# A hybrid encoder trunk: on-chip tiles in a new order, TensorE's operands first and at multiples of 2 KB

## The chip, the cores and the metric

One core of one Trainium2 chip. The metric is device time of one execution in microseconds, as the median of several runs. The kernel and its reference compute in float32; products are made of two float32r parts (a high part and the remainder), which TensorE multiplies.

## The reference

Two layers over 256 tokens of width 1,024. What bears on the time is the chain of matrix products:

```python
def hybrid_layer(x, layer_idx, norm1_g, w_in, ...):
    h = rms_norm(x, norm1_g)
    proj = jnp.einsum('bsd,de->bse', h, w_in)        # 1024 x 10000
    ...
    y_a = mlstm_branch(aq, ak, av, ao, ag, a_conv_w, a_gate_bias, a_norm_g)
    y_b = gqa_branch(bq, bk, bv, b_qnorm_g, b_knorm_g)
    y_c = natten_branch(cq, ck, cv, c_rpb)
    y_d = diff_branch(dq, dk, dv, d_lq1, d_lk1, d_lq2, d_lk2, d_subln_g, lambda_init)
    g = jax.nn.sigmoid(gl.astype(F32)).reshape(bsz, s, N_BRANCH, D_MODEL)
    merged = (g[:, :, 0] * (y_a @ w_up_a) + g[:, :, 1] * (y_b @ w_up_b)
              + g[:, :, 2] * (y_c @ w_up_c) + g[:, :, 3] * (y_d @ w_up_d))
    x = x + merged.astype(dt) @ w_out
    h2 = rms_norm(x, norm2_g)
    ffn = (jax.nn.silu(h2 @ w_ffn_gate) * (h2 @ w_ffn_up)) @ w_ffn_down   # 2816 wide
    return x + ffn
```

After the second layer comes a last RMSNorm.

## The kernel before

All weights come from one array in the order in which they are used (`unit_order`, line 57), in units of 128 x 2,048 float32 that are loaded as halves of 128 x 1,024. A half is loaded by SP's queue into one of four `raw` tiles (`load_next`, line 242), copied by ScalarE with rounding to float32r into one of five `whi` tiles (`emit_hi`, line 258), and VectorE subtracts to leave the remainder in one of five `wlo` tiles (`emit_lo`, line 265). The activations are kept transposed in the same two parts: `xT` (line 208) holds the normalised input as [part, 8 k-slices, 256 tokens], so that its 128 x 128 slices lie 512 bytes apart in a partition; the `yt_` tiles (line 190) do the same for the branches' results and the hidden layer of the feed-forward part.

A product is `mm3` (line 357): high x high, high x low, low x high, three matmuls that add up in one bank. The activation slice is the stationary operand and 512 columns of `whi` or `wlo` are the moving one. `blk512` (line 371) goes over the four k-slices of each unit for both halves of the tokens; `ffn_gu` and `ffn_dn` (lines 1289, 1305) run it over the 11 feed-forward chunks of 256; `bkv_block` (line 1106) multiplies by 272 columns at a time, the first 272 columns of a half and then the next. Between the products small tasks run: transposes on TensorE against `ident`, softmax pieces (`soft_item`, line 739, whose operands are `rq_` and `kb` tiles; `soft_tail`, line 849, with `re_` as moving and `vb` or `vc` as stationary operand), the mLSTM heads (`a_head`, line 604, with `w2_` tiles).

The order of all instructions is written out by the program when it is built. A planner (`Track` and `Meter`, lines 103 to 167) adds up estimated times for each engine, from the shapes of the operands (lines 146 to 156) and from which parts of which tile, by its name and the offset within it, were written or read before (lines 112 to 129). `slot` (line 296) asks it which task may go next. Tiles of the same kind are handed out from lists (`Res`, line 81), oldest free one first. Line 166 is the one place from which `Meter` issues, so nearly every instruction in the profile has that line, and tiles are what tells them apart; the loads have line 240.

All on-chip tiles are declared at the head of `trunk`, lines 186 to 227, and once more at line 447 (`stats`). They take their places in a partition in this order, each beginning at a multiple of 32 bytes:

```python
    W2 = many(8, "w2_", [128, 520])
    K4 = many(4, "k4_", [128, 1024])
    YT = many(3, "yt_", [128, 2, 4, S], F32R)
    ...
    xT = sb("xT", [128, 2, 8, S], F32R)
    ...
    raw = [sb("raw%d" % i, [128, 1024]) for i in range(NRAW)]
    whi = [sb("whi%d" % i, [128, 1024], F32R) for i in range(NH)]
    wlo = [sb("wlo%d" % i, [128, 1024], F32R) for i in range(NH)]
```

Of the kernel before, what the change touches and what calls it, by code (L numbers as in the profile page):

```python
# [12 lines left out]
F32R = mybir.dt.float32r  # L13
BF16 = mybir.dt.bfloat16
# [5 lines left out]
S = 256  # L20
D = 1024
# [149 lines left out]
def trunk(ctx: ExitStack, tc, x_in, wts, par, parc, cst, dist, t2w, fg, out):  # L171
# [8 lines left out]
    def sb(name, shape, dt=F32):  # L180
        return pool.tile(shape, dt, name=name, tag=name)

    def many(n, name, shape, dt=F32):
        return Res([sb("%s%d" % (name, i), shape, dt) for i in range(n)])

    dense = [psp.tile([128, 512], F32, name="pd%d" % i, tag="pd%d" % i) for i in range(3)]
    PS = Res([psp.tile([128, 512], F32, name="pa%d" % i, tag="pa%d" % i) for i in range(5)])
    W2 = many(8, "w2_", [128, 520])
    K4 = many(4, "k4_", [128, 1024])
    YT = many(3, "yt_", [128, 2, 4, S], F32R)  # L190
    RQ = many(2, "rq_", [128, 2, 512], F32R)
    RE = many(3, "re_", [128, 2, 512], F32R)
    T2 = many(2, "t2_", [128, 2, 384])
    SM = many(8, "sm_", [128, 16])
    acc = [sb("acc%d" % i, [128, 2, 512]) for i in (0, 1)]
    EA = Res(acc)
    everyres = [EA, PS, W2, K4, YT, RQ, RE, T2, SM]

    ident = sb("ident", [128, 128])
    make_identity(nc, ident)  # L200
    identr = sb("identr", [128, 36], F32R)
    cs = sb("cs", [128, K_W])
    mA = sb("mA", [128, 384])
    ndist = sb("ndist", [128, 384], BF16)
    mhalf = sb("mhalf", [128, 20])
    lnsc = sb("lnsc", [128, 1])
    x = sb("x", [128, 2, D])
    xT = sb("xT", [128, 2, 8, S], F32R)
    pt = sb("pt", [128, P_W])
    pc2 = [sb("pc%d" % i, [128, C_W]) for i in range(L)]  # L210
    rowz = sb("rowz", [128, 2, 2, 36])
    iz = sb("iz", [128, 2, 36])
    mrow = sb("mrow", [128, 2, S], F32R)
    gcols = sb("gcols", [128, 2, 2, 36])
    gtok = sb("gtok", [128, 32])
    va = sb("va", [128, 2, 4, 129])
    vd = sb("vd", [128, 2, 512])
    vc = sb("vc", [128, 2, 8, 2, 64], F32R)
    vb = sb("vb", [128, 2, 2, 2, 64], F32R)
    ktok = sb("ktok", [128, 2, 128])  # L220
    kb = sb("kb", [128, 2, S], F32R)
    bsm = sb("bsm", [128, 2, 10])
    mvt = sb("mvt", [128, 16])
    NRAW, NH = 4, 5
    raw = [sb("raw%d" % i, [128, 1024]) for i in range(NRAW)]
    whi = [sb("whi%d" % i, [128, 1024], F32R) for i in range(NH)]
    wlo = [sb("wlo%d" % i, [128, 1024], F32R) for i in range(NH)]

    with tc.manual_schedule():

# [6 lines left out]
        def dma(eng, dst, src):  # L237
            state["dma"] = max(state["dma"], track.after(None, [], [dst])) + math.prod(dst.shape) / 94e3
            track.note(None, [], [dst], state["dma"] + 2.3)
            eng.dma_start(dst, src)  # L240

        def load_next():
            h = state["load"]
            if h < nhalf:
                w = width(h)
                dma(nc.sync, raw[h % NRAW][:, :w], wts[h // 2][:, (h % 2) * 1024:(h % 2) * 1024 + w])
                state["load"] += 1
                if h >= NRAW and consts:
                    dma(nc.sync, *consts.pop(0))
# [175 lines left out]
        for _ in range(NRAW - 2):  # L425
            load_next()
        dtile = W2.get()
        consts += [(pt[:, :], par[0]), (cs[:, :], cst), (dtile[:, :384], dist),
# [8 lines left out]
        def tables():  # L437
# [5 lines left out]
            V.tensor_scalar(ndist, dtile[:, :384], -1.0, None, op0=ALU.mult)  # L443
            W2.put(dtile)

# [4 lines left out]
        def boundary_chunk(t, c, gcol, st):  # L450
# [16 lines left out]
            yield  # L467
            while not W2.ok(1):
                yield
            w = W2.get()  # L470
            A.activation(w[:, :512], x[:, t, c * 512:(c + 1) * 512], AF.Square,
                         accum_out=st[:, 2 * c + t:2 * c + t + 1])
            W2.put(w)
            bnd["sq"] += 1
# [24 lines left out]
        def y_up(b, y):  # L499
            while not yt_ok(b):  # L500
                yield
            yt = yt_get(b)
            for t in (0, 1):
                while not PS.ok(1):
                    yield
                p = PS.get()
                for k in range(4):
                    T.transpose(p[:, k * 128:(k + 1) * 128], y[:, t, k * 128:(k + 1) * 128], ident)
                yield
                p4 = p.rearrange("p (k n) -> p k n", k=4)  # L510
                A.activation(yt[:, 0, :, tsl(t)], p4, AF.Copy)
                yield
                sub_lo(yt[:, 1, :, tsl(t)], p4, yt[:, 0, :, tsl(t)])
                PS.put(p)
            yield
            Bs[b]["yt"] = yt
# [87 lines left out]
        def a_head(B, h, pc):  # L604
# [61 lines left out]
            yield  # L666
            while not (PS.ok(2) and ("hb" in B or K4.ok(1))):
                yield
            if "hb" not in B:
                B["hb"] = K4.get()  # L670
            ps = (PS.get(), PS.get())
# [34 lines left out]
        def a_main(B, pc):  # L706
# [28 lines left out]
            yield from y_up("a", hb.rearrange("p (t n) -> p t n", t=2))  # L735
            K4.put(hb)


        def soft_item(B, i, kind):
# [46 lines left out]
            if kind == "c":  # L786
                T2.put(B["t2"].pop(i))
            yield
# [40 lines left out]
            yield  # L829
            while not (PS.ok(1) and "v" in B and ("y" in B or K4.ok(1))):  # L830
                yield
            if "y" not in B:
                B["yraw"] = K4.get()
                B["y"] = B["yraw"].rearrange("p (t n) -> p t n", t=2)
# [14 lines left out]
        def soft_tail(B, i, c, e):  # L849

            while not (PS.ok(1) and RE.ok(1)):
                yield
            p, r = PS.get(), RE.get()
            for kt in (0, 1):
# [16 lines left out]
            for kt, half in ((0, 0), (0, 1), (1, 1), (1, 0)):  # L871
# [3 lines left out]
                else:  # L875
                    T.matmul(p[:, 0:256], v[kt].rearrange("p a n -> p (a n)"), r[:, 0, k2], start=kt == 0, stop=kt == 1)
            RE.put(r)
            yield
# [141 lines left out]
        def c_main(l, B):  # L1020
# [10 lines left out]
            for i in range(4):  # L1031
                while not T2.ok(1):
                    yield
                t2 = T2.get()
                dma(nc.scalar, t2[:, :, :], t2w[l, i])
# [467 lines left out]
```

## Time and profile before

| | |
|---|---|
| median of 3 runs | 1092.74 us (1091.99 to 1093.77) |
| the profiled execution | 1093.29 us |
| its span, first to last instruction | 1091.5 us, 14,727 instructions |
| TensorE, matmuls | busy 1077.9 us (99%), 5,272 instructions |
| TensorE, weight loads | 879.6 us (81%), beside the matmuls |
| VectorE | 765.2 us (70%) |
| ScalarE | 616.8 us (57%) |
| GpSimd | 156.6 us (14%) |
| DMA | 184.8 MB, mean 169 GB/s |

The page gives busy time by engine, the span in 40 slices, the chain of work that ended last and the groups of instructions; the trace answers for a stretch, an engine or a tile. Matmuls overlap in the records: the duration of one runs until its result has left the array, while the next has long begun. How fast they follow one another is seen in the timeline, from one start to a later one with the instructions between them counted.

### The profile page before, as it was taken

The numbers are of one execution on the slowest core, as the hardware profiler recorded it, in microseconds if no ns is written. First come the engines' busy times: TensorE is split into PE (matmuls) and PEld (weight loads), VectorE is DVE, ScalarE is ACT, GpSimd is POOL, SyncE is SP. The second block draws the span as 40 slices with busy tenths as digits, with TensorE's granted clock in tenths as the row PEclk, the third lists the DMA queues.
The fourth block names the chain that finished last, engine by engine and source line by source line (L and its number), as shares of the span: only waits on it lengthen the run. The fifth ranks groups of instructions, "written<-read, shape, count | busy, mean of one in ns | idle before, by whom it ended". The sixth has DMA issues, their size and how long they took to land.

```text
span 1091.5 us, 14727 instructions
## 1 busy us (share of the span) xinstructions
PE 1077.9 (99%) x5272; PEld 879.6 (81%) x5272; DVE 765.2 (70%) x1361; ACT 616.8 (57%) x1095; POOL 156.6 (14%) x130
## 2 busy tenths in 40 slices
PE   9999999999999999999999999999999999999997
PEld 7888887888888888888788888787888888888885
DVE  6689889787556755564576988997965666556555
ACT  7665657775444644444467656686744464444443
POOL 0001345143300000000000006434223000000000
PEclk9999999999999999999999999999999999999999
DMA  8444444545555555545554444345365546564551
GB/s 286 156 163 157 155 135 146 165 135 188 178 175 173 190 192 177 193 171 178 184 166 136 163 166 143 127 165 171 128 200 185 179 169 196 173 206 158 193 182 68
DMA packets 52328, 184.80 MB, mean 169 GB/s; under 512 B 6048, under 2 KB 6432, under 8 KB 52256
## 3 DMA queue, kind: packets, MB, share of 16 engines
q1 hardware_dynamic: 50112, 178.57, 49.1%
q10 hardware_dynamic: 2144, 5.31, 1.6%
q8 instruction: 41, 0.67, 0.2%
q14 instruction: 31, 0.25, 0.1%
HBM read 182.80 MB, written 1.05 MB: 168 GB/s over the span
## 4 chain that ended last, share of the span: by engine, by line
PE 95%; DVE 3%; DMA 1%; issue 0%; ACT 0%; POOLq 0%; POOL 0%; ACTq 0%
PE pd L166 69%; PE pa L166 26%; DVE sm L166 1%; DVE wlo L166 1%; DVE k L166 1%; DMA x<-in_x_dram 1%; DVE rq L166 0%; DVE acc L166 0%; ACT yt L166 0%; DVE mvt L166 0%; ACT pa L166 0%; DVE x L166 0%; ACT k L166 0%; POOLq L1499 0%; POOL st L166 0%
## 5 line engine op out<-in xcount | busy, mean ns | idle before, releaser
L166 PE MATMUL pd<-whi,xT 128*128 128x512 f32 (+1 forms) x1984 | 646.4, 396 | 0.0
L166 DVE TENSOR_TENSOR wlo<-raw,whi 128x1024 fp32r<-128x1024 f32 (+2 forms) x341 | 426.5, 1263 | 113.5 <-ACT whi L166 112.9
L166 PEld LDWEIGHTS pd<-whi,xT 128*128 128x128 f32 x1984 | 372.1, 188 | 85.1
L166 ACT ACTIVATE whi<-raw 128x1024 fp32r<-128x1024 f32 (+2 forms) x341 | 354.1, 1047 | 147.0 <-PE pd L166 95.7
L166 PE MATMUL pd<-wlo,xT 128*128 128x512 f32 (+1 forms) x992 | 389.8, 393 | 0.0
L166 PEld LDWEIGHTS pd<-wlo,xT 128*128 128x128 f32 x992 | 187.0, 188 | 39.4 <-DVE wlo L166 0.3
L166 PE MATMUL pa<-whi,yt 128*128 128x512 f32 x408 | 138.5, 401 | 1.4 <-ACT yt L166 1.4
L166 PEld LDWEIGHTS pa<-whi,yt 128*128 128x128 f32 x408 | 76.6, 188 | 19.6 <-ACT yt L166 1.8
L166 PE MATMUL pd<-whi,yt 128*128 128x512 f32 (+1 forms) x272 | 87.1, 390 | 0.0
L166 PE MATMUL pa<-wlo,yt 128*128 128x512 f32 x204 | 80.5, 394 | 0.0
L166 DVE SCALAR_TENSOR_TENSOR w<-w,pd 128x256 f32<-128x256 f32 x44 | 18.5, 421 | 88.3 <-ACT w L166 88.2
L166 POOL TENSOR_TENSOR st<-st,mhalf 128x2 f32<-128x2 f32 (+1 forms) x6 | 3.9, 654 | 521.2 <-DVE st L166 521.2
L166 ACT ACTIVATE k<-pd,st 128x512 f32<-128x512 f32 (+1 forms) x52 | 31.5, 624 | 58.7 <-PE pd L166 58.7
L166 PEld LDWEIGHTS pd<-whi,yt 128*128 128x128 f32 x272 | 50.7, 188 | 10.9
L166 ACT ACTIVATE w<-pd,st 128x256 f32<-128x256 f32 (+1 forms) x48 | 23.6, 492 | 54.8 <-PE pd L166 52.4
L166 ACT ACTIVATE yt<-pa 128x512 fp32r<-128x512 f32 x34 | 20.3, 597 | 58.6 <-PE pa L166 58.6
L166 PE MATMUL pd<-wlo,yt 128*128 128x512 f32 (+1 forms) x136 | 52.7, 388 | 0.0
L166 PEld LDWEIGHTS pa<-wlo,yt 128*128 128x128 f32 x204 | 38.5, 189 | 7.9
L166 POOL TENSOR_TENSOR w<-w,sm 128x512 f32<-128x512 f32 x32 | 40.5, 1290 | 23.9 <-DVE sm L166 23.9
L166 POOL TENSOR_TENSOR acc<-acc,k 128x512 f32<-128x512 f32 x16 | 30.5, 1907 | 85.0 <-DVE k L166 85.0
L166 DVE TENSOR_TENSOR yt<-pa,yt 128x512 fp32r<-128x512 f32 x30 | 20.6, 688 | 28.9 <-ACT yt L166 28.9
L166 ACT ACTIVATE w<-w,sm 128x256 f32<-128x256 f32 x64 | 31.7, 501 | 11.0 <-DVE sm L166 6.3
(154 smaller groups left out, 1010.8 us busy)
## 6 DMA issues: line engine op xcount, KB each, us to landing
raw<-in_wts_dram SPq DMA_DIRECT2D x332, 512.0 KB, 3.7
t<-in_t2w_dram ACTq DMA_DIRECT2D x8, 384.0 KB, 3.6
raw<-in_wts_dram SPq DMA_DIRECT2D x8, 272.0 KB, 2.9
pt<-in_par_dram SPq DMA_DIRECT2D x1, 584.0 KB, 7.6
pt<-in_par_dram ACTq DMA_DIRECT2D x1, 584.0 KB, 4.6
out_dram<-k SPq DMA_DIRECT2D x2, 288.0 KB, 2.1
x<-in_x_dram ACTq DMA_DIRECT2D x1, 512.0 KB, 9.1
k<-in_fg_dram ACTq DMA_DIRECT2D x1, 512.0 KB, 3.5
```

Source lines behind the costliest of these rows:

```text
L166: return f(out, *a, **k)
```

## The change

The declarations at the head of `trunk` are put in another order. First come three small tiles (`ndist`, `rowz`, `gcols`), then the weights in two parts, `xT`, and the other tiles that TensorE reads, then the larger tiles of the other engines and last the small ones. The `w2_` tiles become 512 columns wide in place of 520. Nothing but declarations is changed.

```diff
     PS = Res([psp.tile([128, 512], F32, name="pa%d" % i, tag="pa%d" % i) for i in range(5)])
-    W2 = many(8, "w2_", [128, 520])
-    K4 = many(4, "k4_", [128, 1024])
+    NRAW, NH = 4, 5
+
+    ndist = sb("ndist", [128, 384], BF16)
+    rowz = sb("rowz", [128, 2, 2, 36])
+    gcols = sb("gcols", [128, 2, 2, 36])
+    whi = [sb("whi%d" % i, [128, 1024], F32R) for i in range(NH)]
+    wlo = [sb("wlo%d" % i, [128, 1024], F32R) for i in range(NH)]
+    xT = sb("xT", [128, 2, 8, S], F32R)
     YT = many(3, "yt_", [128, 2, 4, S], F32R)
     RQ = many(2, "rq_", [128, 2, 512], F32R)
     RE = many(3, "re_", [128, 2, 512], F32R)
+    mrow = sb("mrow", [128, 2, S], F32R)
+    vc = sb("vc", [128, 2, 8, 2, 64], F32R)
+    vb = sb("vb", [128, 2, 2, 2, 64], F32R)
+    kb = sb("kb", [128, 2, S], F32R)
+    vd = sb("vd", [128, 2, 512])
+    acc = [sb("acc%d" % i, [128, 2, 512]) for i in (0, 1)]
+    K4 = many(4, "k4_", [128, 1024])
+    W2 = many(8, "w2_", [128, 512])
+    x = sb("x", [128, 2, D])
+    raw = [sb("raw%d" % i, [128, 1024]) for i in range(NRAW)]
+    ktok = sb("ktok", [128, 2, 128])
+    ident = sb("ident", [128, 128])
     T2 = many(2, "t2_", [128, 2, 384])
     SM = many(8, "sm_", [128, 16])
-    acc = [sb("acc%d" % i, [128, 2, 512]) for i in (0, 1)]
     EA = Res(acc)
     everyres = [EA, PS, W2, K4, YT, RQ, RE, T2, SM]
 
-    ident = sb("ident", [128, 128])
     make_identity(nc, ident)
     identr = sb("identr", [128, 36], F32R)
     cs = sb("cs", [128, K_W])
     mA = sb("mA", [128, 384])
-    ndist = sb("ndist", [128, 384], BF16)
     mhalf = sb("mhalf", [128, 20])
     lnsc = sb("lnsc", [128, 1])
-    x = sb("x", [128, 2, D])
-    xT = sb("xT", [128, 2, 8, S], F32R)
     pt = sb("pt", [128, P_W])
     pc2 = [sb("pc%d" % i, [128, C_W]) for i in range(L)]
-    rowz = sb("rowz", [128, 2, 2, 36])
     iz = sb("iz", [128, 2, 36])
-    mrow = sb("mrow", [128, 2, S], F32R)
-    gcols = sb("gcols", [128, 2, 2, 36])
     gtok = sb("gtok", [128, 32])
     va = sb("va", [128, 2, 4, 129])
-    vd = sb("vd", [128, 2, 512])
-    vc = sb("vc", [128, 2, 8, 2, 64], F32R)
-    vb = sb("vb", [128, 2, 2, 2, 64], F32R)
-    ktok = sb("ktok", [128, 2, 128])
-    kb = sb("kb", [128, 2, S], F32R)
     bsm = sb("bsm", [128, 2, 10])
     mvt = sb("mvt", [128, 16])
-    NRAW, NH = 4, 5
-    raw = [sb("raw%d" % i, [128, 1024]) for i in range(NRAW)]
-    whi = [sb("whi%d" % i, [128, 1024], F32R) for i in range(NH)]
-    wlo = [sb("wlo%d" % i, [128, 1024], F32R) for i in range(NH)]
```

## Rows read from the trace of the kernel before

**Rows 1.** The page: busy us (share of span) xinstructions; granted clock in tenths

```profile
PE 1077.9 (99%) x5272; PEld 879.6 (81%) x5272; DVE 765.2 (70%) x1361; ACT 616.8 (57%) x1095; POOL 156.6 (14%) x130
...
PEclk9999999999999999999999999999999999999999
```

**Rows 2.** The page: the chain that ended last, shares by engine

```profile
PE 95%; DVE 3%; DMA 1%; issue 0%; ACT 0%; POOLq 0%; POOL 0%; ACTq 0%
```

**Rows 3.** TensorE's groups by form: xcount | busy us, mean ns | idle before

```profile
L166 PE MATMUL pd<-whi,xT 128*128 128x512 f32 x1920 | 632.9, 400 | 0.0
L166 PE MATMUL pd<-wlo,xT 128*128 128x512 f32 x960 | 380.7, 397 | 0.0
L166 PE MATMUL pa<-whi,yt 128*128 128x512 f32 x408 | 138.5, 401 | 1.4 <-ACT yt L166 1.4
...
L166 PE MATMUL pd<-wlo,yt 128*128 128x512 f32 x128 | 50.5, 394 | 0.0
...
L166 PE MATMUL pa<-whi,xT 128*128 128x512 f32 x64 | 21.9, 403 | 0.0
...
L166 PE MATMUL pa<-wlo,xT 128*128 128x512 f32 x32 | 12.7, 397 | 0.0
```

**Rows 4.** The chain in order of time: start us, us, what; feed-forward stretches

```profile
385.65 11.20 PE pd L166 x48
...
1060.62 11.20 PE pd L166 x48
```

**Rows 5.** TensorE's timeline, 299 to 308 us: start us, us, instructions merged

```profile
299.73 0.63 PE L166 MATMUL pd<-whi,xT 128*128 128x512 f32 x2
...
307.43 0.63 PE L166 MATMUL pd<-whi,xT 128*128 128x512 f32 x2
```

**Rows 6.** TensorE's timeline, 286 to 296 us, products with yt

```profile
286.43 0.63 PE L166 MATMUL pd<-whi,yt 128*128 128x512 f32 x2
...
295.53 0.63 PE L166 MATMUL pd<-whi,yt 128*128 128x512 f32 x2
```

**Rows 7.** TensorE's timeline, 244 to 251 us, products with yt

```profile
244.96 0.62 PE L166 MATMUL pd<-whi,yt 128*128 128x512 f32 x2
...
250.53 0.64 PE L166 MATMUL pd<-whi,yt 128*128 128x512 f32 x2
```

**Rows 8.** TensorE's timeline, 51 to 52 us, the key/value block's 272 columns

```profile
51.15 0.28 PE L166 MATMUL pd<-wlo,xT 128*128 128x272 f32 x1
...
51.52 0.28 PE L166 MATMUL pd<-wlo,xT 128*128 128x272 f32 x1
...
51.89 0.29 PE L166 MATMUL pd<-wlo,xT 128*128 128x272 f32 x1
```

**Rows 9.** TensorE's timeline, 243 to 245 us, eight of 256 columns

```profile
243.56 1.10 PE L166 MATMUL pa<-re,vc 128*128 128x256 f32 x8
244.50 0.39 PE L166 MATMUL pd<-whi,yt 128*128 128x512 f32 x1
```

**Rows 10.** TensorE's timeline, twelve score matmuls of two branches

```profile
158.50 0.97 PE L166 MATMUL pa<-kb,rq 64*128 64x256 f32 x12
...
216.93 0.97 PE L166 MATMUL pa<-rq 64*128 64x256 f32 x12
```

**Rows 11.** TensorE's timeline, 220 to 222 us, eight transposes and a product

```profile
220.74 1.04 PE L166 MATMUL pa<-ident,w 128*128 128x128 f32 x8
221.53 0.48 PE L166 MATMUL pd<-whi,xT 128*128 128x512 f32 x1
221.85 0.40 PE L166 MATMUL pd<-wlo,xT 128*128 128x512 f32 x1
```

**Rows 12.** A stretch: us; busy us (x) of PE, PEld, DVE, ACT, POOL; clock

```profile
310.00:546.00 236.00, 235.31 (x1053) 189.95 (x1052) 138.99 (x183) 111.68 (x155) 0.71 (x1) 1.00 0.55 182
```

**Rows 13.** VectorE on the w tiles: ns min/median/max, first and last start

```profile
L166 DVE SCALAR_TENSOR_TENSOR w<-w,pd x44: 420/420/423, 365.7 to 1072.4; 128x256 f32<-128x256 f32 x44
```

**Rows 14.** The page: DMA issues, KB each, median us to landing

```profile
raw<-in_wts_dram SPq DMA_DIRECT2D x332, 512.0 KB, 3.7
t<-in_t2w_dram ACTq DMA_DIRECT2D x8, 384.0 KB, 3.6
```

## The prediction

> **What bounds the kernel now.** I read the page's busy times and clock line first: the reader is to see TensorE busy for 99% of the span, at its upper clock level (2.4 GHz) in all 40 slices, and the chain of work that ended last lying on TensorE for 95% [rows 1, 2]. So only what changes a matmul's pace, or the few microseconds in which TensorE waits, can move the end. The groups by form come next: four of them, 1,920 + 960 + 64 + 32 = 2,976 matmuls of 512 columns, take their stationary operand from `xT`; four more, 408 to 128 strong, 996 together, take it from a `yt` tile; the moving operand is a `whi` or `wlo` half in all 3,972 [rows 3]. Their mean of about 400 ns is no pace, since one begins before the last has ended; pace is read from starts. In the chain every one of 18 feed-forward stretches is 48 matmuls in 11.20 us, which is 233.3 ns each [rows 4], and the timeline shows three of them every 0.70 us, 33 in 7.70 us, 233.3 ns again [rows 5]. So 3,972 x 233.3 ns = 927 us of the 1,078 busy ones hang on this one figure.
>
> At 2.4 GHz and one column a cycle 512 columns are 213.3 ns: each of these matmuls takes 20.0 ns too long. That is what a layout could be after. 3,972 x 20.0 ns = 79 us is the most that there is to win, and the question is whether addresses have to do with it.
>
> **The change part by part.** *What it removes and adds.* No instruction. Line 188's `w2_` tiles lose columns 512 to 519, which nothing reads or writes: their slices end at 512 at the latest. The planner (lines 120 to 156) takes its costs from shapes and its overlaps from a tile's name and the offset within the tile, and no order in the lists of free tiles is changed. So the same instructions come in the same order on every engine and queue, with the same waits: no step passes another, nothing new is queued behind a wait. Only addresses differ. Cost: 0.
>
> *What moves.* Tiles lie one after another in order of declaration, each at a multiple of 32 bytes, and in the program as it is built the first begins at byte 16,512 of a partition. Adding up sizes: before, `whi` and `wlo` begin at 256 in their 2 KB, `xT` at 672, `yt`, `rq`, `re` at 384, `kb` at 96, the `w2_` tiles at 128, 160, ... 352, `raw` at 256. After it, `ndist`, `rowz` and `gcols` (768 + 576 + 576 bytes) bring the sum to 18,432 = 9 x 2,048, and from there all tiles up to `ktok` are whole multiples of 2 KB, so the edit does what it says (`ident` alone, read in transposes, begins at 1 KB). A 512-column operand then fills one 2 KB piece instead of parts of two.
>
> *A read that runs over a 2 KB line.* Three rows show what that costs. In the feed-forward and gate blocks every second `xT` slice (672 + 1,024) runs over a line and its neighbours don't; each three matmuls still take 0.70 us [rows 5]. In the key/value block the moving reads of 272 columns begin at 256 (inside) and 1,344 (over the line) in turn: from one `wlo` row to the next lie twice the inside kind and once the other, then the reverse, and both are 0.37 us [rows 8]; a cost of 20 ns for a line would part them by 20 ns, and the rows resolve 10. I take 0.
>
> *Where a read begins.* The excess goes by columns: 512 columns 20.0 ns; 272 columns 123.3 - 113.3 = 10.0 ns [rows 8]; 256 columns of `re`, 0.94 us for eight, 117.5 - 106.7 = 10.8 ns [rows 9]. That is 0.039, 0.037 and 0.042 ns a column, with starts at 256, 320 and 384 modulo 512. An excess that grows with the columns read and is the same for three starts is no price of a start. Transposes of 128 columns, which the planner counts at two cycles a column (106.7 ns), take (1.11 - 0.23) / 8 = 109.6 ns [rows 11]: 2.9 ns over, so the engine can go near its full pace, and the excess belongs to the one-cycle form. None of the rows begins at 0, though, so a full gain isn't excluded; its bounds are 0 and -79 us. I take 0, the value of the nearest rows.
>
> *Small effects of the stationary operand's start.* Matmuls on `yt` (384, a multiple of 64 bytes) aren't quite as regular as those on `xT` (672, not one): one stretch has 39 in 9.10 us, 233.3 ns [rows 6], another 24 in 5.57 us, 232.1 ns [rows 7]. With `xT` at a multiple of 64 too, its 2,976 may go as `yt`'s do. Bounds: 0 and 2,976 x -1.2 ns = -3.6 us. I take the mean of both stretches by count, 14.67 us / 63 = 232.9 ns: 2,976 x -0.47 ns = -1.4 us.
>
> *Other engines.* They can only matter where TensorE waits. The additions on VectorE that read and write `w2_` tiles, whose eight starts are multiples of 32 bytes and only half of them of 64, take 420 ns at least, at the median, and 423 at most [rows 13]: the start is worth nothing there. In the stretch from 310 to 546 us TensorE was busy for 235.3 of 236 us with VectorE at 59% and ScalarE at 47% [rows 12], and its 11.20 us repeated: what the others read and write at the same moment, in tiles next to the one being multiplied, doesn't show either. Bounds -0.5 to +0.5 us, taken as 0. Here a rule of the Trainium skill speaks against the change. SBUF — State Buffer, section "Who interferes with whom", says that engines meet at ports and at nothing else, and that TensorE waits for no other engine; [rows 12] agree, and by that rule a new layout is worth 0.
>
> *DMA.* The 384 KB loads of `t2`, into tiles at 384, land after 3.6 us, the 512 KB loads of `raw`, at 256, after 3.7 [rows 14]; the waits for weights are hidden anyway. Only `x` at the start lies in the open, 1% of the chain; bounds -0.5 to +0.2 us, taken as 0.
>
> *Sum.* The profiled execution took 1093.29 us, span 1091.5 and 1.8 around it; it lies 0.55 above the median of 1092.74. 1093.29 - 1.4 = 1091.9 for such an execution, 1091.3 for the median.
>
> **The rivals.**
> *Every matmul takes the best stretch's pace* (faster). If a common start of both operands is what [rows 7] owe their 232.1 ns to, all 3,972 gain 1.2 ns: -4.8 us, 1088.0. For it: the figure exists in the trace. Against: the same operands from the same tiles ran at 233.3 in [rows 6].
> *The full pace* (much faster). If a start at 0 frees the matmul of its excess down to the transposes' 2.9 ns, 3,972 x 17.1 = -67.9 us: 1024.8. Against: the same excess a column for three starts. The Trainium skill would put that pace at 215.7 ns between starts of 512 columns (TensorE: Matmul & The Clock Gate, "Wait — 56ns, not 53.3ns?"), an estimate by that page of 3,972 x -17.6 = -69.9 us; this trace has no such row, and the measured 233.3 decides.
> *Equal starts collide* (slower). TensorE loads the next weights while it streams the moving operand. Today the two begin at different places modulo 512 bytes (256 against 160 or 384); afterwards both at 0. If reads that begin alike get in each other's way, each of the 3,972 pays. Against: where `rq` is both operands, they begin alike (1,408 against 384, the same modulo 512), with `kb` they don't (96 against 384), and twelve matmuls busy the engine for 0.97 us either way [rows 10]. These rows resolve 10 ns in twelve, 0.8 ns each, 1.7 for 512 columns: up to +6.6 us, 1099.3. It decides from 0.6 ns a matmul on.
> *The edit doesn't do what it says*: excluded by the addresses above.
>
> **How the numbers follow.** Forecast (order and pace kept, `xT` a little quicker): 0.72, own range 1089.1 (all of `xT` at 232.1) to 1094.0 (no gain, and the spread of 1.0 above the median that the three times show). Best pace everywhere: 0.13. Full pace: 0.04. Collision: 0.11. A measurement of this kernel tells about 0.2% (2.2 us) from no change, so the limits are 1090.5 and 1094.9. The forecast gives 0.67 to the middle, 0.04 to faster, 0.01 to slower: faster 0.04 + 0.13 + 0.04 = 0.21, same 0.67, slower 0.12. The range takes in the forecast and the first rival with 1 us below it, and the lower part of the collision: 1087.0 to 1098.0; full pace and most of the collision, some 0.13, are left out.
>
> **What would show it right or wrong.** In the profile after: the same 14,727 instructions and the same counts in every form; 48 matmuls in 11.20 us still, or 11.15 and less if `xT` gains; 272 columns still at about 123 ns and 256 at 117.5; VectorE's and ScalarE's means unchanged. Wrong would be a pace of 512 columns clearly under 232 (alignment was the excess), or over 234 (collision), or another order of instructions.

## The result, and the profile after

| | before | after |
|---|---|---|
| median | 1092.37 us (1091.22 to 1093.77) | 1073.2 us (1071.05 to 1074.44) |
| the profiled execution | 1093.29 us, span 1091.5 | 1072.2 us, span 1070.4 |
| 512-column matmuls, mean from start to start | 233.29 ns (3,681 spacings) | 227.82 ns (3,684 spacings) |

The ratio is 0.9822 [0.98, 0.9844]: the change makes the kernel 19.2 us faster, where 1.4 us had been forecast and where the range ended at 1087.0. The third line of the table is worked out from the starts of neighbouring matmuls of 512 columns that lie less than 260 ns apart. It accounts for the whole gain: 3,972 x (233.29 - 227.82) = 21.7 us, beside 21.1 us by which the span became shorter.

The page of after, busy us (share of the span) by engine and the granted clock in tenths, to be read against [rows 1], and the shares of the chain, against [rows 2]:

```profile
PE 1055.4 (99%) x5272; PEld 877.0 (82%) x5272; DVE 761.2 (71%) x1361; ACT 616.7 (58%) x1095; POOL 156.5 (15%) x130
...
PEclk9999999999999999999999999999999999999999
...
PE 95%; DVE 3%; DMA 1%; issue 0%; ACT 0%; ACTq 0%; POOLq 0%; POOL 0%
```

The counts are the same to the instruction, each engine's instructions come in the same order in both traces, the clock is at its upper level (2.4 GHz) in all slices as before, and TensorE still sets the end. Its busy time shrank by 22.5 us, VectorE's by 4, ScalarE's by 0.1. TensorE's groups by form (xcount | busy us, mean ns) show where, against [rows 3]:

```profile
L166 PE MATMUL pd<-whi,xT 128*128 128x512 f32 x1920 | 623.0, 395 | 0.0
L166 PE MATMUL pd<-wlo,xT 128*128 128x512 f32 x960 | 374.7, 391 | 0.0
L166 PE MATMUL pa<-whi,yt 128*128 128x512 f32 x408 | 137.0, 397 | 1.4 <-ACT yt L166 1.4
```

All forms of 512 columns lost 3 to 6 ns in the mean. As before the mean of one is no pace; the chain and the timeline give that. In the chain in order of time (start us, us, what) the 48 matmuls of a feed-forward stretch take 10.88 us in place of the 11.20 of [rows 4], 226.7 ns each, in 18 stretches (two more, the first of each layer, take 10.92):

```profile
377.31 10.88 PE pd L166 x48
...
1040.07 10.88 PE pd L166 x48
```

The timeline (start us, us, instructions merged) shows three matmuls on `xT` every 0.68 us, 39 in 8.84 us, and three on `yt` likewise, 36 in 8.16 us: 226.7 ns in both, against 233.3 in [rows 5, 6] and 232.1 in [rows 7]:

```profile
291.17 0.61 PE L166 MATMUL pd<-whi,xT 128*128 128x512 f32 x2
...
300.01 0.61 PE L166 MATMUL pd<-whi,xT 128*128 128x512 f32 x2
```

```profile
280.29 0.61 PE L166 MATMUL pd<-whi,yt 128*128 128x512 f32 x2
...
288.45 0.61 PE L166 MATMUL pd<-whi,yt 128*128 128x512 f32 x2
```

Narrower forms did not gain. Matmuls of 272 columns still come three in 0.37 us [rows 8], eight of 256 columns of `re` take 0.92 us after 0.94 [rows 9], and twelve score matmuls 0.97 or 0.98 us [rows 10]:

```profile
50.05 0.29 PE L166 MATMUL pd<-wlo,xT 128*128 128x272 f32 x1
...
50.42 0.29 PE L166 MATMUL pd<-wlo,xT 128*128 128x272 f32 x1
```

```profile
238.47 1.09 PE L166 MATMUL pa<-re,vc 128*128 128x256 f32 x8
239.39 0.40 PE L166 MATMUL pd<-whi,yt 128*128 128x512 f32 x1
```

```profile
161.43 0.98 PE L166 MATMUL pa<-kb,rq 64*128 64x256 f32 x12
...
212.03 0.97 PE L166 MATMUL pa<-rq 64*128 64x256 f32 x12
```

So the gain belongs to one form, 512 columns, and is there on `xT` and `yt` alike. What about their addresses gives it?

### The profile page after: what moved, and what is told of

It reads as the page before. It is cut to its first block, busy times and chain, and to the rows that moved or that the text cites. A ratio compares the mean times of both kernels' runs of the same rounds, so it can differ in the third digit from the quotient of the medians.

```text
span 1070.4 us, 14727 instructions
## 1 busy us (share of the span) xinstructions
PE 1055.4 (99%) x5272; PEld 877.0 (82%) x5272; DVE 761.2 (71%) x1361; ACT 616.7 (58%) x1095; POOL 156.5 (15%) x130
## 4 chain that ended last, share of the span: by engine, by line
PE 95%; DVE 3%; DMA 1%; issue 0%; ACT 0%; ACTq 0%; POOLq 0%; POOL 0%
PE pd L166 69%; PE pa L166 26%; DVE sm L166 1%; DMA x<-in_x_dram 1%; DVE wlo L166 1%; DVE k L166 1%; DVE rq L166 0%; DVE acc L166 0%; ACT yt L166 0%; ACTq L241 0%; DVE mvt L166 0%; ACT pa L166 0%; DVE x L166 0%; ACT k L166 0%; POOLq L1500 0%
## 5 line engine op out<-in xcount | busy, mean ns | idle before, releaser
L166 PE MATMUL pd<-whi,xT 128*128 128x512 f32 (+1 forms) x1984 | 636.6, 391 | 0.0
L166 PE MATMUL pd<-wlo,xT 128*128 128x512 f32 (+1 forms) x992 | 384.0, 387 | 0.0
```

The source lines that it names most:

```text
L166: return f(out, *a, **k)
```

## The experiments

In the expectations, A is the theory that the start of the moving operand itself counts (a read of 2,048 bytes that fills one 2 KB piece is quick); B, that what counts is how the starts of the moving and the stationary operand stand to each other (the first expectations take it modulo 512 bytes); C, that something else in the new layout gives the gain, such as the order of the tiles or which of them are neighbours. Starts are given in bytes. Before, `whi` and `wlo` begin at 256 in their 2 KB, `xT` at 672 and `yt` at 384; after, all of them at 0.

**A table of starts.** A kernel that computes none of the reference: 64 rows of 24 matmuls of 512 columns with 128 x 128 weights, each with its own weight load, eight starts of the stationary tile times eight of the moving one.

```diff
+MOV = (("ma", 0), ("mb", 32), ("mc", 64), ("md", 128), ("me", 256), ("mf", 512), ("mg", 1024), ("mh", 1280))
+STA = (("sa", 0), ("sb", 32), ("sc", 64), ("sd", 128), ("se", 256), ("sf", 384), ("sg", 672), ("sh", 1024))
+        for s in sta:
+            for m in mov:
+                for k in range(REP):
+                    nc.tensor.matmul(pd[i % 2], sta[s], mov[m], start=k == 0, stop=k == REP - 1)
+                i += 1
```

> This kernel computes none of the reference and returns zeros: it runs 64 rows of 24 matmuls (128x128 stationary, 512 moving columns, float32r), each row with one moving tile (ma to mh, beginning at 0, 32, 64, 128, 256, 512, 1024, 1280 within 2 KB) and one stationary tile (sa to sh, beginning at 0, 32, 64, 128, 256, 384, 672, 1024), while the other engines are idle. Theory A, the start of the moving operand sets the pace: 226.7 ns from start to start in the rows of ma, 233.3 in those of me, whatever the stationary tile. Theory B, what counts is that both operands begin at the same place modulo 512 bytes: 226.7 for ma with sa, me with se, mf with sa, and about 233 where the two differ. Theory C, where in the partition the tiles lie (low or high addresses) and not where they begin: one pace in all 64 rows. Theory D, the pace depends on what other engines do at the same time: one pace in all rows, near 216 ns.

Its timeline has one line a row of the table; a row's pace is the next line's start less its own, over 24:

```profile
20.53 5.60 PE L49 MATMUL pd<-ma,sa 128*128 128x512 f32 x24
25.97 5.77 PE L49 MATMUL pd<-mb,sa 128*128 128x512 f32 x24
31.57 5.67 PE L49 MATMUL pd<-mc,sa 128*128 128x512 f32 x24
...
70.05 5.61 PE L49 MATMUL pd<-mb,sb 128*128 128x512 f32 x24
75.50 5.77 PE L49 MATMUL pd<-mc,sb 128*128 128x512 f32 x24
...
264.51 5.75 PE L49 MATMUL pd<-me,sf 128*128 128x512 f32 x24
270.11 5.76 PE L49 MATMUL pd<-mf,sf 128*128 128x512 f32 x24
...
309.32 5.77 PE L49 MATMUL pd<-me,sg 128*128 128x512 f32 x24
314.94 5.76 PE L49 MATMUL pd<-mf,sg 128*128 128x512 f32 x24
```

Both at 0: 5.44 us, 226.7 ns. The moving one at 32, the stationary at 0: 5.60 us, 233.3. Both at 32: 5.45 us, 227.1, so a start at 0 isn't needed. The kernel before has the pairs `me,sf` (weights 256, `yt` 384) with 5.60 us and `me,sg` (weights 256, `xT` 672) with 5.62, 233.3 and 234.2 ns: the slow kind, both of them. From the single starts (the fifth to the last of a row, to leave out its beginning) the whole table, in ns:

| stationary \ moving | 0 | 32 | 64 | 128 | 256 | 512 | 1024 | 1280 |
|---|---|---|---|---|---|---|---|---|
| 0 | 226.7 | 233.3 | 228.9 | 232.7 | 228.0 | 226.7 | 226.7 | 226.7 |
| 32 | 233.4 | 226.7 | 233.3 | 233.2 | 233.0 | 233.4 | 233.4 | 233.4 |
| 64 | 233.5 | 233.1 | 226.7 | 228.7 | 233.5 | 233.5 | 233.5 | 233.5 |
| 128 | 232.0 | 234.5 | 233.2 | 226.7 | 233.6 | 233.6 | 233.6 | 233.6 |
| 256 | 227.8 | 233.3 | 228.9 | 232.7 | 228.0 | 226.6 | 226.6 | 226.6 |
| 384 | 232.5 | 234.0 | 233.5 | 227.9 | 233.6 | 233.6 | 233.6 | 233.6 |
| 672 | 233.6 | 233.6 | 234.3 | 233.2 | 233.6 | 233.5 | 233.5 | 233.5 |
| 1024 | 227.7 | 233.3 | 228.9 | 232.7 | 228.0 | 226.7 | 226.7 | 226.7 |

226.6 to 228.0 ns stand where both starts are equal modulo 256 bytes, and nowhere else; the rest is 228.7 to 234.5, and 41 of the 64 rows lie above 230. That is B with 256 bytes as its period, in place of the 512 expected, and A falls: moving at 0 is slow with a stationary operand at 32, 64, 128, 384 or 672. C and D as this expectation has them, low or high addresses and the work of other engines, wanted one pace in all rows and fall too; the other engines were idle here.

**Everything at 256.** The kernel after with an unused tile of 256 bytes ahead of the weights, so that no operand begins at a multiple of 2 KB, and all begin alike.

```diff
+    shift = sb("shift", [128, 64])
     whi = [sb("whi%d" % i, [128, 1024], F32R) for i in range(NH)]
```

> The changed kernel with one unused tile of 256 bytes ahead of the weights: weights, xT, yt and all the others begin at 256 within 2 KB, in the same order. A (start of the moving operand): back to 233.3 ns a matmul of 512 columns, 48 in 11.20 us, 1092 us. B (common start of both): 226.7 ns and 1073 us stay. C (low addresses, the order): 1073 us.

1072.14 us, ratio to before 0.982 [0.9801, 0.9839]. **The weights alone at 256**, by small tiles moved ahead of and behind them, with everything else at 0:

```diff
+    smt = [sb("sm_%d" % i, [128, 16]) for i in range(4)]
     whi = [sb("whi%d" % i, [128, 1024], F32R) for i in range(NH)]
     wlo = [sb("wlo%d" % i, [128, 1024], F32R) for i in range(NH)]
+    t2t = [sb("t2_0", [128, 2, 384])]
+    ident = sb("ident", [128, 128])
+    smt += [sb("sm_%d" % i, [128, 16]) for i in range(4, 8)]
```

> The changed kernel with four small tiles moved ahead of the weights and 4,864 bytes of small tiles between the weights and xT: whi and wlo begin at 256, xT, yt and the rest at 0 as in the changed kernel. A (start of the moving operand): 233.3 ns a matmul, 1092 us. B (common start): 233.3 ns or a little less, 1090 to 1092 us. C (the order): 226.7 ns, 1073 us.

1072.05 us, ratio 0.9819 [0.98, 0.9838]. Both keep the whole gain. No 2 KB piece is filled by a moving read in either, so A falls in the kernel as well; and the second has starts that are equal modulo 256 and not modulo 512, which settles the period: by 512 bytes, as B then stood, 1090 to 1092 us had been expected. C, the order, expected what came in both, and is left for the runs below.

**The weights at 0 in the kernel before.** `pc1` and `bsm` declared behind `wlo`, so that the weights begin at a multiple of 2 KB while `xT` stays at 672 and `yt` at 384.

```diff
-    pc2 = [sb("pc%d" % i, [128, C_W]) for i in range(L)]
+    pc2 = [sb("pc0", [128, C_W])]
...
-    bsm = sb("bsm", [128, 2, 10])
...
     wlo = [sb("wlo%d" % i, [128, 1024], F32R) for i in range(NH)]
+    pc2 += [sb("pc1", [128, C_W])]
+    bsm = sb("bsm", [128, 2, 10])
```

> The kernel before with two small tiles (pc1, bsm) moved behind the weights: raw, whi and wlo begin at 0 within 2 KB, high in the partition as before; xT (672), yt, rq, re (384) stay where they were. A (start of the moving operand): 226.7 ns, 1073 us. B (common start): 233 ns, 1090 to 1092 us. C (the order, low addresses): 233.3 ns, 1092 us.

1091.65 us, ratio 1.0004 [0.9994, 1.0015]; its chain, in order of time, has 11.20 us for 48 matmuls, as in [rows 4]:

```profile
385.66 11.20 PE pd L166 x48
```

The moving operands at multiples of 2 KB are worth nothing by themselves.

**The gain taken back.** The kernel after with 96 unused bytes between the weights and `xT`: same order, same neighbours, and the weights still at 0; `xT` and all behind it begin 96 bytes further on.

```diff
     wlo = [sb("wlo%d" % i, [128, 1024], F32R) for i in range(NH)]
+    apart = sb("apart", [128, 24])
     xT = sb("xT", [128, 2, 8, S], F32R)
```

> The changed kernel with one unused tile of 96 bytes between the weights and xT: weights begin at 0, xT, yt, rq, re and all behind them at 96 within 256 bytes; order and places otherwise as in the changed kernel. B (common start modulo 256): 233.3 ns a matmul of 512 columns, 48 in 11.20 us, 1091 to 1093 us. C (the order, low addresses): 226.7 ns, 1072 us.

1094.65 us, ratio 1.0024 [1.0013, 1.0034]. Its chain:

```profile
384.78 11.25 PE pd L166 x48
```

Ninety-six bytes take back the whole gain and a little more: 48 matmuls take 11.25 us, 234.4 ns each, where the two later tables have 234.0 for a moving start of 0 and a stationary one of 96. The order of the tiles, all of it kept, holds none of the gain, so C falls too.

**The gain without the change's order.** The kernel before with three unused tiles, so that `yt` begins at 256, `xT` at 768 and the weights at 512: no multiple of 2 KB, and equal modulo 256. The `w2_` tiles are 512 wide, as after the change.

```diff
-    W2 = many(8, "w2_", [128, 520])
+    W2 = many(8, "w2_", [128, 512])
     K4 = many(4, "k4_", [128, 1024])
+    pad0 = sb("pad0", [128, 32])
     YT = many(3, "yt_", [128, 2, 4, S], F32R)
...
+    pad1 = sb("pad1", [128, 56])
     xT = sb("xT", [128, 2, 8, S], F32R)
...
+    pad2 = sb("pad2", [128, 40])
     raw = [sb("raw%d" % i, [128, 1024]) for i in range(NRAW)]
```

> The kernel before, its order of tiles kept, with three unused tiles of 128, 224 and 160 bytes ahead of yt, xT and raw (and w2 512 wide to make room): yt, rq and re begin at 256, xT at 768, whi and wlo at 512 within 2 KB, so all are the same modulo 256 and none at a multiple of 2 KB. B (common start modulo 256): 226.7 ns a matmul, 1072 to 1074 us. C (the order) and A (multiples of 2 KB): 233.3 ns, 1092 us.

1072.83 us, ratio 0.982 [0.98, 0.9839]; in the chain:

```profile
379.16 10.88 PE pd L166 x48
```

Some 512 bytes of padding do all that the new layout does. **`xT` alone** is the same with `pad1` of 24 columns ahead of `xT` and `pad2` behind it: `xT` at 768, the weights at 512, `yt` left at 384.

```diff
+    pad1 = sb("pad1", [128, 24])
     xT = sb("xT", [128, 2, 8, S], F32R)
+    pad2 = sb("pad2", [128, 40])
```

> The kernel before with an unused tile of 96 bytes ahead of xT and one of 160 behind it: xT begins at 768 and the weights at 512 within 2 KB, the same modulo 256; yt, rq and re stay at 384, which is not. B: the 2,976 matmuls on xT go at 226.7 ns (48 in the feed-forward stretches in 10.88 us), the 996 on yt stay at about 233; three quarters of 19.3 us are gained, 1077 us. C: 1092 us.

1076.98 us, ratio 0.9853 [0.9834, 0.9873]: 15.9 us of the 20.1 that its neighbour with three pads gains. By count `xT` has 2,976 of the 3,972, 75%; it got 79%. By spacings it had more to gain: from before to after those on `xT` fall from 233.5 to 227.8 ns in the mean and those on `yt` from 232.6 to 228.1, which gives `xT` 17.0 of 21.5 us, 79% as well. Within one execution the two kinds now stand side by side: in the chain 48 matmuls on `xT` take 10.89 to 10.93 us in 18 of 20 stretches, 226.9 to 227.7 ns each, and in the timeline those on `yt`, still unequal, come like this:

```profile
303.20 0.62 PE L166 MATMUL pd<-whi,yt 128*128 128x512 f32 x2
...
305.29 0.62 PE L166 MATMUL pd<-whi,yt 128*128 128x512 f32 x2
...
307.38 0.64 PE L166 MATMUL pd<-whi,yt 128*128 128x512 f32 x2
```

From 303.20 to 307.38 lie 18 matmuls: 232.2 ns each.

**How near is equal, and which matmuls.** A second kernel that computes none of the reference: thirty rows of 24 matmuls as above; twelve with the stationary slice 0 to 252 bytes into its tile and the moving operand at 0, six with fewer stationary columns, twelve with fewer moving columns.

```diff
+ROWS = ([("ma", 512, n, 128, e) for n, e in (("sa", 0), ("sb", 1), ("sc", 2), ("sd", 4), ("se", 12), ("sf", 24), ("sg", 44),
+                                             ("sh", 48), ("si", 52), ("sj", 56), ("sk", 60), ("sl", 63))]
+        + [("mb", 512, n, c, e) for n, c, e in (("sa", 96, 0), ("sb", 64, 0), ("sc", 32, 0),
+                                                ("sd", 96, 24), ("se", 64, 24), ("sf", 32, 24))]
+        + [("mc", w, n, 128, e) for w, n, e in ((448, "sa", 0), (448, "sb", 24), (384, "sc", 0), (384, "sd", 24),
...
+                nc.tensor.matmul(pd[i % 2][0:c, 0:w], sta[s][:, e:e + c], mov[m][:, 0:w], start=k == 0, stop=k == REP - 1)
```

> This kernel computes none of the reference and returns zeros: 30 rows of 24 matmuls in float32r with the other engines idle. Rows of ma: stationary slices that begin 0, 4, 8, 16, 48, 96, 176, 192, 208, 224, 240 and 252 bytes behind the moving operand's start modulo 256. Rows of mb: 512 moving columns with 96, 64 and 32 stationary columns, at 0 and at 96 bytes. Rows of mc: 448, 384, 320, 256, 192, 128 moving columns with 128 stationary ones, at 0 and at 96 bytes. Theory B2 (the weight load and the moving read get in each other's way, and least when both begin at the same place modulo 256 bytes): 226.7 ns at 0, about 233.5 at 4 to 176 and 208 to 252, about 229 at 192; with fewer stationary columns both fall, and the gap of 6.8 ns between 0 and 96 with them (3.4 at 64 columns, 1.7 at 32). Theory E (the moving read alone is slow, by 13.3 ns a 512 columns, and only the rest depends on the common start): at 0 the pace stays at 226.7 for any number of stationary columns. By moving columns B2 expects the excess over 1/2.4 ns a column to stay much the same while the load still fits in beside the read (down to 256); E expects it to fall with the columns.

```profile
18.75 5.63 PE L47 MATMUL pd<-ma,sa 128*128 128x512 f32 x24
24.21 5.74 PE L47 MATMUL pd<-ma,sb 128*128 128x512 f32 x24
29.79 5.70 PE L47 MATMUL pd<-ma,sc 128*128 128x512 f32 x24
...
74.46 5.62 PE L47 MATMUL pd<-ma,sk 128*128 128x512 f32 x24
79.92 5.61 PE L47 MATMUL pd<-ma,sl 128*128 128x512 f32 x24
85.36 5.69 PE L47 MATMUL pd<-mb,sa 128*96 128x512 f32 x24
90.89 5.68 PE L47 MATMUL pd<-mb,sb 128*64 128x512 f32 x24
96.40 5.72 PE L47 MATMUL pd<-mb,sc 128*32 128x512 f32 x24
101.97 5.77 PE L47 MATMUL pd<-mb,sd 128*96 128x512 f32 x24
```

One element is enough: with the stationary slice 4 bytes behind the moving start a row takes 29.79 - 24.21 = 5.58 us (232.4 ns by the single starts; at 8 bytes 230.6, at 16 to 224 bytes 230.1 to 234.0). In the other direction it isn't: at 240 and 252, which is 16 and 4 bytes short of the next equal place, 226.7 ns; at 224, 32 bytes short, 233.4. Nor does the difference alone order the unequal starts: 192 bytes on, about 229 was expected, as the first table has with the moving start at 64 or 128 (228.7 to 228.9), but with the moving start at 0 it is 233.3. The columns came out in a way that was not expected:

| | starts equal | stationary 96 bytes on |
|---|---|---|
| 512 moving, 128 stationary columns | 226.6 ns | 234.0 ns |
| 512 moving, 96 stationary | 230.0 | 233.5 |
| 512 moving, 64 stationary | 230.0 | 231.6 |
| 512 moving, 32 stationary | 231.7 | 230.4 |
| 448 moving, 128 stationary | 202.5 | 200.0 |
| 384 moving, 128 stationary | 173.3 | 173.3 |
| 320 moving, 128 stationary | 146.6 | 146.7 |
| 256 moving, 128 stationary | 119.7 | 117.5 |
| 192 moving, 128 stationary | 111.8 | 111.9 |
| 128 moving, 128 stationary | 111.6 | 111.8 |

Theory E, by which equal starts keep 226.7 ns for any number of stationary columns, falls with the 230.0 at 96. A collision of two reads (B2) should have grown less as the weight load grew shorter (its records go from 188 to 108 ns over these rows). At unequal starts it does, from 234.0 to 230.4; at equal starts the pace grows longer, to 231.7. So 226.7 is a state that wants both the equal start and the full 128 columns, and what lies between is 230 to 234. And at 448 moving columns and fewer equal starts gain nothing: 384, 320 and 256 columns take 384/2.4 + 13.3, 320/2.4 + 13.3 and 256/2.4 + 10.8 to 13.0 ns, and at 192 and 128 the pace no longer falls with the columns.

**Which two reads.** The weights of the next matmul are loaded while the present one streams its moving operand. In a row of one pair both loads come from the same tile, so the tables can't say whether a matmul's own weights or those loaded beside it have to begin alike. A third kernel, which again computes none of the reference, alternates pairs (in its trace a weight load of some 188 ns begins 1 to 4 ns behind each matmul's start); in its names the letter is the row.

```diff
+# a row: the pairs (moving tile, stationary tile) ...: 0 at 0, 1 at 96, 2 at 512 bytes
+ROWS = [("a", ("00",), 512), ("b", ("01",), 512), ("c", ("00", "11"), 512), ("d", ("01", "10"), 512),
+        ("e", ("00", "01"), 512), ("f", ("00", "10"), 512), ("g", ("00", "00", "02"), 512), ("h", ("01",), 512),
+        ("i", ("00",), 512), ("j", ("00",), 496), ("k", ("01",), 496), ("l", ("00",), 480), ("m", ("01",), 480),
+        ("n", ("00", "01", "10"), 512), ("o", ("00", "01", "11", "10"), 512)]
```

> Computes none of the reference: fifteen rows of 24 matmuls, each with its own weight load, of operands whose starts are set by hand (0, 96 or 512 bytes into 2 KB); the output is zeros. The pace is read from the starts. Question: which two reads have to begin alike for the quick pace of 226.7 ns? In a row of one pair the stationary operand of a matmul and that of the next one are the same tile, so the tables so far can't tell. Row c takes (moving 0, stationary 0) and (96, 96) in turn: each matmul is equal with its own weights and unequal with the weights loaded next. Row d takes (0, 96) and (96, 0) in turn: unequal with its own, equal with the next. Theory P (a matmul's own two operands count): c 226.7, d 233.4 ns. Theory N (the moving read meets the load of the next matmul's weights, which runs beside it): c 233.4, d 226.7. Both: rows a, g, i (equal throughout; g with a stationary start of 512 among them) 226.7, rows b and h (0, 96) 233.4; row e (moving 0, stationary 0 and 96 in turn) and f (moving 0 and 96, stationary 0) between, near 230, as half of their pairs are equal by either. A third theory H (a row's pace depends on what ran before it, not on its pair): h and i differ from b and a by over 1 ns. Columns: 496 and 480 columns at equal starts 220.0 and 213.3 (fixed 13.3 ns over 512, 496 and 480 columns at one column in 1/2.4 ns), at unequal starts 226.7 and 220.0 if the addition of 6.7 ns is a fixed one; 220.0 and 213.3 if it comes only with a read of 512 columns.

```profile
28.58 5.63 PE L54 MATMUL pd<-ma,sa 128*128 128x512 f32 x24
34.05 5.78 PE L54 MATMUL pd<-mb,sb 128*128 128x512 f32 x24
39.66 5.77 PE L54 MATMUL pd<-mc,sc 128*128 128x512 f32 x24
45.27 5.68 PE L54 MATMUL pd<-md,sd 128*128 128x512 f32 x24
50.79 5.69 PE L54 MATMUL pd<-me,se 128*128 128x512 f32 x24
...
89.04 5.36 PE L54 MATMUL pd<-ml,sl 128*128 128x480 f32 x24
94.23 5.37 PE L54 MATMUL pd<-mm,sm 128*128 128x480 f32 x24
99.44 5.75 PE L54 MATMUL pd<-mn,sn 128*128 128x512 f32 x24
105.03 5.78 PE L54 MATMUL pd<-mo,so 128*128 128x512 f32 x24
```

| row | pairs (moving, stationary) | own starts equal | next weights' equal | ns |
|---|---|---|---|---|
| a, i | (0, 0) | all | all | 226.9 |
| b, h | (0, 96) | none | none | 234.0 |
| c | (0, 0), (96, 96) | all | none | 233.8 |
| d | (0, 96), (96, 0) | none | all | 229.7 |
| e | (0, 0), (0, 96) | half | half | 229.9 |
| f | (0, 0), (96, 0) | half | half | 230.0 |
| g | (0, 0), (0, 0), (0, 512) | all | all | 228.0 (226.7 from the tenth on) |
| n | (0, 0), (0, 96), (96, 0) | a third | a third | 232.5 |
| o | (0, 0), (0, 96), (96, 96), (96, 0) | half | none | 235.2 |

Rows c and o are what tells: in c every matmul has its own two operands alike, in o every second one, and they are as slow as the row with none. Theory P falls. Row d, where only the weights loaded beside it are alike, is quicker than b by 4.3 ns, though not all the way to 226.9: N has its direction from rows c, d and o (e, f, g and n fit both theories), and misses 3 ns in d, where 224 and 236 ns take turns. So a matmul's own weights alone give nothing and the next ones alone 4.3 of the 7.1 ns; what the rest wants, no row tells. H falls, since h repeats b and i repeats a to 0.1 ns. For the columns, equal and unequal starts give 220.0 and 223.4 ns at 496, and 216.4 and 216.7 at 480 (5.19 and 5.21 us a row above): the difference of 7 ns at 512 is gone 32 columns below it. Neither expectation for the columns said that.

No experiment found a pace under 226.6 ns at 512 columns, and three layouts within 1.2 us of the kernel after share it; none of the layouts tried is clearly faster.

## Why the prediction was wrong, point by point

**What held.** The bound was read rightly: the time hangs on the pace of 3,972 matmuls, and it was that pace that moved, with the clock level, the order and the counts of before. The edit did to the addresses what was worked out. A read over a 2 KB line costs nothing: in the kernel with everything at 256 every moving read runs over one, at 1072.14 us. VectorE and ScalarE and the transfers moved by nothing that reaches the end.

**The step that failed is "Where a read begins",** taken at 0 from bounds of 0 and -79 us. It reasoned that the excess over one column a cycle grows with the columns and is the same for three starts, so that no start can be its cause. Both halves were drawn from rows that could not show the effect. The 272 and 256 columns of [rows 8, 9] have fewer columns than the 480 at which equal starts gain no more than 0.3 ns; their excess of some 10 to 13 ns is a part that the tables show at all widths from 256 columns up, at equal starts too, and not half of the 20.0 ns at 512. The 20.0 ns are 13.3 that equal starts leave and 6.7 by the starts; two terms were read as one that is proportional. And the three starts compared were those of the moving operand alone. What counts is how they stand to the stationary ones, and in each row of 512 columns before that was unequal: 0 against 160 (`xT`) and 0 against 128 (`yt`) modulo 256. "None of the rows begins at 0" was the right doubt about the wrong quantity; the rows lacked an equal pair, not a zero.

**The rival "Equal starts collide"** had the right pair of reads, the next weights and the moving operand, and the wrong sign: it is the unequal starts that are slow. Its counter-evidence was a pair of rows with `rq` as both operands and with `kb` [rows 10]: 64 rows high and 256 columns wide. At 256 columns of full height the second kernel has equal starts 2.2 ns slower, not quicker, so rows of that width could not tell what 512 columns do. The 6.6 us that those rows left open were for the wrong form.

**"Every matmul takes the best stretch's pace"** took the 232.1 ns of [rows 7] for the sign of a common start. In the table a stationary start 128 bytes off the moving one, as `yt` has it, gives 232.0 to 233.6 ns: 232.1 is one of the paces of the slow kind. The 226.7 of an equal pair stood nowhere in the trace of before. The term of -1.4 us, `xT` going as `yt` does, came from the same rows; before, the spacings on `yt` are indeed shorter (232.6 ns, 890 of them, against 233.5, 2,736), but that a multiple of 64 bytes is the cause isn't shown: with 96 bytes between the weights and `xT` both begin at 96, no multiple of 64, and have 234.0 and 234.1. **"The full pace"** went too far: at equal starts 13.3 ns a matmul stay, 53 us over the kernel, and no layout tried touched them.

**What size it should have had.** From the table, unequal less equal is 233.6 - 226.7 = 6.9 ns, 3,972 x 6.9 = 27.4 us; the kernel got 21.7. Most of the rest lies at the beginnings of stretches. After another form has run, the first four spacings of after are 231.6 ns in the mean (604 of them), the next five 229.1 (517), and from the tenth on 226.7 (2,563); before, they are 233.4, 233.3 and 233.3. Those first nine cost 604 x 5.0 + 517 x 2.4 = 4.3 us of the 5.7 that are missing; another 1.2 is the kernel's slow pace of 233.3 in place of the table's 233.6. In the timeline of after, behind four transposes that begin at 312.95 us, three matmuls take 0.70, 0.69 and then 0.68 us:

```profile
313.85 0.63 PE L166 MATMUL pd<-whi,xT 128*128 128x512 f32 x2
...
314.55 0.63 PE L166 MATMUL pd<-whi,xT 128*128 128x512 f32 x2
...
315.24 0.62 PE L166 MATMUL pd<-whi,xT 128*128 128x512 f32 x2
...
315.92 0.39 PE L166 MATMUL pd<-whi,xT 128*128 128x512 f32 x1
```

The quick pace is one that a stream of equal matmuls settles into. It isn't another form alone that interrupts it: in the first table, all of one form, a row of equal starts behind a row of equal starts is quick at once (`mf,sa`), and behind an unequal row it takes from one spacing (`mb,sb`) to ten (`md,sf`).

**What stays open.** Shown is the condition (equal starts modulo 256 bytes or the stationary one up to 16 bytes short of it, full 128 x 128 weights, nearly 512 columns, up to about ten matmuls to settle), and that the start of the next weights is needed for it, by rows c and o; by row d it isn't enough alone. Not shown is what happens inside: a plain collision doesn't explain why fewer stationary columns lose the quick pace at equal starts, nor the 229.7 of row d. Nor is the origin of the remaining 13.3 ns known; no run here leaves the weight load out.

## What to carry to other kernels

Where a TensorE-bound kernel streams 512 columns of float32r through changing 128 x 128 weights, let moving and stationary operands, the slices of the tiles included, begin at the same place modulo 256 bytes; three pads of 512 bytes in all gave 1.8% here, and neither the order nor multiples of 2 KB are needed for it. One tile of odd size declared between the two kinds takes it all back, so look at starts again whenever tiles are added. And before an excess is called proportional from narrower forms, or independent of an address from starts of one operand, ask whether the rows hold a case in which the suspected condition is met.

## What the runs showed of the hardware that was not expected

- The pace of 512-column float32r matmuls with a weight load each is 226.7 ns when the moving start equals the stationary start modulo 256 bytes and mostly 233 to 234 ns otherwise; 4 bytes too far lose it, 4 or 16 bytes too short do not, and 32 too short do (233.4). The Trainium skill (SBUF — State Buffer, "Who interferes with whom") gives TensorE two read ports, one for the moving operand and one for the weight load, and calls them independent. These runs differ: a matmul's pace hangs on how the starts of the two reads stand to each other, and the measurement decides.
- With full 128 x 128 weights the difference is one of nearly full reads: 7.1 ns at 512 columns, 3.4 at 496, 0.3 at 480, none at 384 and 320, and at 448 and 256 equal starts are even 2 ns slower.
- Even the quick pace keeps 13.3 ns over one column a cycle, 512/2.4 = 213.3 ns (from 320 to 512 columns the pace grows by 80.0 ns, which is one column in 1/2.4 ns). The Trainium skill (TensorE: Matmul & The Clock Gate, "Wait — 56ns, not 53.3ns?") has about 2.5 ns there for matmuls back to back; in these runs, with a weight load for each matmul, it is 13.3 at 320, 384, 496 and 512 columns and 16 at 448 and 480, and the measurement decides.
- The quick pace has to be reached: behind another form the kernel after shows 231.6 ns for four spacings, 229.1 for the next five and 226.7 from the tenth on, and behind unequal starts of the same form a table row takes one to ten.
